# Forgetting attention's values in two 64-column halves for the low probabilities, memory values by 512 queries

## The chip, the cores and the metric

The kernel runs on one core of one Trainium2 chip. The metric is the device time of one execution in microseconds. Before the change it is 1254.17 us, the median of three runs (1252.7 to 1254.45).

## The reference

Two decoder layers over 1024 tokens of width 1024. Each layer projects its input once to a main branch, a memory query and two gates, mixes, and applies an output projection, a residual and a LayerNorm. Layer 0's main branch is causal pooling with windows 2, 4, 8 and 16 and a 256 x 256 map per group. Layer 1's is forgetting attention, 16 heads of 64 over keys, values and forget gates projected from its input. Both layers have 4-head cross-attention into 256 memory tokens.

```
# forgetting attention, per block of 128 queries
logits = einsum('bqhd,bkhd->bhqk', qi, k) * scale + (ci[..., :, None] - cum_k[:, :, None, :])
p = softmax(where(mask, logits, -inf))
out = einsum('bhqk,bkhd->bqhd', p, v)
# memory attention
p = softmax(einsum('bshd,bmhd->bhsm', q, mk) * MEM_HEAD_DIM ** -0.5)
out = einsum('bhsm,bmhd->bshd', p, mv)
# each layer
y = concatenate([y_main * silu(g_main), y_mem * silu(g_mem)]) @ w_out
x = layer_norm(ALPHA * x + y, g, b)
```

All inputs and outputs are f32.

## The kernel before

**Split operands.** Every f32 operand of a matmul is split into a high and a low part, and a product is taken in three matmuls: high by high, high by low, low by high. Projections use two f32r parts (`hi_lo`, L138). Attention probabilities and values use two f16 parts after scaling (`scaled_halves` L239 for values, `halves` L752 for probabilities), and the scale is undone when the result leaves PSUM (`undo`, `un`).

**Stages.** In order: pooling group 0 (`pool_group`, L488), memory keys and values of layer 0 (`mem_kv`), memory attention of layer 0 (`mem_attention`, L267), pooling groups 1 to 3, output projection and LayerNorm of layer 0, then for layer 1 memory keys, values and attention, `start_units` (the first head pairs' projections and the forget gates), the forgetting attention `fox` (L810), and the output projection.

**What sets the order on TensorE.** In the memory attention and in layer 1's attention the order of TensorE is the program's own (`manual_schedule`); the other engines are ordered by a scheduler. A projection is a generator (`slab`, L170) that yields after each matmul of 128 x 512; `Fill.pump(cols)` draws from such generators until the given number of columns has been issued. So attention work that waits for softmax stands between stretches of projection work. In `mem_attention` the fill is the four memory gates, in `fox` the gates and the next pairs' keys, queries and values.

**Memory attention.** For each step t (128 queries) `probs` makes the logits of four heads, softmax on VectorE and ScalarE, and a DMA transpose of the two f16 parts into `pt[t]` (tag "T", six buffers). `values(c, h)` covers 256 queries: for each of two tiles six matmuls (two blocks of memory tokens, three products), accumulated in a PSUM tile of tag "O" (h = 1) or "T", which VectorE scales into `ys[h]` (L324). It runs at t = 3, 5, 7, 9, with fill between the heads. At the end `ys` is multiplied by the gates (L338).

**Pooling.** After a group's two gates `pool_group` applies the group's map: four accumulators of 512 columns, six matmuls each, tag "pj" with two banks, the same that the gates before use. VectorE multiplies each by scale and gate (L530).

**Forgetting attention.** For each head the eight query tiles are done from the last to the first (`tile_of`). `probs` (L708) makes logits and exponentials of one tile, `halves` the two f16 parts one step later, and `turn` (L763) transposes them by DMA into `pt[hd, i]`: the first i + 1 blocks are the high part, the next i + 1 the low part. `values(hd, c, o)` (L773) runs LAG = 5 steps later, twice a head: c = 1 for tiles 4 to 7 (26 blocks of keys in all), c = 0 for tiles 0 to 3 (10 blocks). The weights `v[:, b, 2j : 2j + 2, :]` hold the 64 columns of V's high part beside the 64 of its low part. Each block is multiplied twice, by the high and by the low probabilities, so all four products are in one PSUM bank ("O", one buffer), 64 rows for V's high part and 64 for V's low part. ScalarE scales one half (L787), VectorE adds the other (L788). `VALUES` (L39) tells the pacing how many columns such a call takes, at which step of a head.

**`start_units`** (L686): 48 units of pair 0's projections (the key slab), `v_first` (values of the first two pairs and the forget logits, 192 matmuls at L606), the gates' VectorE work, transposes of values with 24 units between them, the rest of pair 0, then pair 1 with the two TensorE steps of the gates (L637 to L645).

Of the kernel before, what the change touches and what calls it, by code (L numbers as in the profile page):

```python
# [15 lines left out]
ALU = mybir.AluOpType  # L16
AX = mybir.AxisListType

P = 128
# [3 lines left out]
ST = S // P  # L23
NH = 512
HEADS = 16
MH = 4
# [9 lines left out]
LAG = 5  # L36
APART = 6 * NH
PSCALE = 2.0 ** 15
VALUES = {0: 52 * P, 4: 20 * P}  # L39


class Fill:
# [29 lines left out]
def trunk_kernel(ctx, tc, x, xT, memT, win, wk, wv0, wv, wmk, wmv, wout, poolw, pscale, lng, lnb, bforget, out):  # L72
# [28 lines left out]
    def ps(shape, tag, bufs):  # L101
        return psum.tile(shape, F32, tag=tag, name=nm(tag), bufs=bufs)
# [164 lines left out]
    def mem_attention(l, XH, XL, kv, qtile, ytile, yd):  # L267

        (kh, kl, v, undo), keys, vals = kv
        qs = []  # L270
        if l:
            for h in range(MH):
                keys(h)
        for h in range(MH):
            qh, ql = qtile(), qtile()
            run(slab(win[l, 8 + h], XH, XL, lambda cols, acc: hi_lo(qh[:, cols], ql[:, cols], acc)))
            qs.append((qh, ql))
            if not l:
                keys(h)
            vals(h)  # L280
        ys, gs = [ytile() for _ in range(MH)], [G() for _ in range(MH)]
        pt, fill = {}, Fill()
        for h in range(MH):
            fill.add(gate_units(win[l, 20 + h], gs[h], XH, XL), SLAB)

        def probs(i):

            p, two = sb([P, MH, NMEM], "P", 4), sb([P, 2, MH, NMEM], "P", 4, F16)
            m, ms, sm, r = tiny(MH), tiny(MH), tiny(MH), tiny(MH)
            for hp in range(2):  # L290
                lg = ps([P, 2, NMEM], "L", 3)
                for j in range(2):
                    h = 2 * hp + j
                    qh, ql = (t[:, i * P : (i + 1) * P] for t in qs[h])
                    mm3(lg[:, j, :], ((qh, kh[:, h, :]), (qh, kl[:, h, :]), (ql, kh[:, h, :])))
                pair = slice(2 * hp, 2 * hp + 2)
                nc.vector.tensor_reduce(m[:, pair], lg, AX.X, ALU.max, negate=True)
                nc.vector.tensor_scalar(ms[:, pair], m[:, pair], MSCALE, None, ALU.mult)
                for j in range(2):
                    h = 2 * hp + j  # L300
                    nc.scalar.activation(
                        p[:, h, :], lg[:, j, :], AF.Exp, bias=ms[:, h : h + 1], scale=MSCALE, accum_out=sm[:, h : h + 1],
                    )
            nc.vector.tensor_scalar(r, sm, 1.0 / PSCALE, None, ALU.mult)
            nc.vector.reciprocal(r, r)
            for h in range(MH):
                nc.scalar.activation(two[:, 0, h, :], p[:, h, :], AF.Copy, scale=r[:, h : h + 1])
                nc.vector.scalar_tensor_tensor(
                    two[:, 1, h, :], p[:, h, :], r[:, h : h + 1], two[:, 0, h, :], ALU.mult, ALU.subtract,
                )  # L310
            pt[i] = T([P, 2, MH, 2, P], F16)
            nc.sync.dma_start_transpose(
                pt[i].rearrange("p e h m q -> p (e h m) q"), two.rearrange("p e h t -> p (e h t)"),
            )

        def values(c, h):
            acc = ps([P, 2 * P], *(("O", 1) if h == 1 else ("T", 2)))
            for j in range(2):
                t = pt[2 * c + j]
                mm3(acc[:, j * P : (j + 1) * P], [  # L320
                    (v[:, h, 2 * e + m, :], t[:, f, h, m, :])
                    for m in range(2) for e, f in ((0, 0), (0, 1), (1, 0))
                ])
            nc.vector.tensor_scalar(ys[h][:, c * 2 * P : (c + 1) * 2 * P], acc, undo[:, h : h + 1], None, ALU.mult)  # L324

        with tc.manual_schedule(engines={PE}):
            for t in range(ST + 2):
                part = fill.left / (5 * (ST + 2 - t))
                if t < ST:
                    probs(t)  # L330
                fill.pump(part if t <= ST else 3 * part)
                for h in range(MH):
                    if t >= 3 and t % 2 == 1:
                        values((t - 3) // 2, h)
                    fill.pump(part if t <= ST else part / 2)
            fill.pump(float("inf"))
        for h in range(MH):
            nc.vector.tensor_tensor(ys[h], ys[h], gs[h], ALU.mult)  # L338
            nc.sync.dma_start(yd[:, h, :], ys[h])
# [143 lines left out]
    with tc.tile_pool(name="in0", bufs=1) as in0:  # L483

        def bt():
            return sb([P, S], "B", 8, F32R, in0)

        def pool_group(g):  # L488
            w = WINDOWS[g]
            pms = []  # L490
            for f in (2 * g, 2 * g + 1):
                u = sb([P, S], "P", 4)
                run(slab(
                    first[f] if g == 0 else win[0, f], XH, XL, lambda cols, acc: nc.scalar.copy(u[:, cols], acc),
                    ("L", 3) if f == 1 else ("pj", 2),
                ))
                cur, sh = u, 1
                while sh < w:
                    nxt = G()
                    nc.vector.tensor_tensor(nxt[:, sh:], cur[:, sh:], cur[:, : S - sh], ALU.add)  # L500
                    nc.vector.tensor_copy(nxt[:, :sh], cur[:, :sh])
                    cur, sh = nxt, 2 * sh
                pm = G()
                nc.vector.scalar_tensor_tensor(pm[:, w - 1 :], cur[:, w - 1 :], 1.0 / w, u[:, w - 1 :], ALU.mult, ALU.subtract)
                nc.vector.tensor_tensor(pm[:, : w - 1], cur[:, : w - 1], invc[:, : w - 1], ALU.mult)
                nc.vector.tensor_tensor(pm[:, : w - 1], pm[:, : w - 1], u[:, : w - 1], ALU.subtract)
                ph, pl = T(), T()
                hi_lo(ph, pl, pm)
                pms.append((ph, pl))
            r = raw([P, 2, 2 * P])  # L510
            nc.sync.dma_start(r, poolw[g])
            wh, wl = (MK([P, 2, 2 * P]) for _ in range(2))
            hi_lo(wh, wl, r)
            ys = []
            for f in (2 * g, 2 * g + 1):
                y = sb([P, S], "Y", 4, F32, in0)
                run(gate_units(win[0, 12 + f], y, XH, XL))
                ys.append(y)
            for d in range(2):
                f = 2 * g + d  # L520
                for n in range(2):
                    acc = ps([P, NH], "pj", 2)
                    terms = []
                    for ct in range(2):
                        a, b = wh[:, ct, d * P : (d + 1) * P], wl[:, ct, d * P : (d + 1) * P]
                        ph, pl = (t[:, n * NH : (n + 1) * NH] for t in pms[ct])
                        terms += [(a, ph), (a, pl), (b, ph)]
                    mm3(acc, terms)
                    yn = ys[d][:, n * NH : (n + 1) * NH]
                    nc.vector.scalar_tensor_tensor(yn, acc, pschalf[:, f : f + 1], yn, ALU.mult, ALU.mult)  # L530
                nc.sync.dma_start(y0d[f // 4, :, f % 4, :], ys[d])

        wtags = [("B", 8)] * 4 + [("W", 4)] * 2 + [("MK", 4)] * 2 + [("Y", 4)] * 2 + [("PG", 0), ("w", 0)]
        out_proj = OutProj(0, w_slots(wtags, in0), y0d)
        pool_group(0)
        kv = mem_kv(0)
        mem_attention(0, XH, XL, kv, bt, lambda: sb([P, S], "Y", 4, F32, in0), y0d[2])
        for g in range(1, 4):
            pool_group(g)
            out_proj.split((4, 12, 12)[g - 1])  # L540

        XH1, XL1 = (sb([P, KT, S], "A", 2, F32R) for _ in range(2))
        out_proj.rest(x, XH1, XL1, x1)
# [3 lines left out]
    with tc.tile_pool(name="in1", bufs=1) as in1:  # L547
# [137 lines left out]

        def start_units(own, following):  # L686

            yield from islice(own, 48)
            yield from v_first()
            gates = forget_gates()  # L690
            next(gates)
# [81 lines left out]
        def values(hd, c, o):  # L773

            (v, un), b = pairs[hd // 2][2], hd % 2
            acc = ps([P, NH], "O", 1)
            for i in range(4 * c, 4 * c + 4):
                mm3(
                    acc[:, (i % 4) * P : (i % 4) * P + P],
                    [  # L780
                        (v[:, b, 2 * j : 2 * j + 2, :].rearrange("p e d -> p (e d)"), pt[hd, i][:, e * (i + 1) + j, :])
                        for j in range(i + 1) for e in range(2)
                    ],
                )
            own, other = slice(64 * b, 64 * b + 64), slice(64 - 64 * b, P - 64 * b)
            oc = o[own, c * NH : (c + 1) * NH]
            nc.scalar.activation(oc, acc[other, :], AF.Copy, scale=un[own])  # L787
# [169 lines left out]
```

## Time and profile before

| | before |
|---|---|
| runs | 1254.17 us median of 3 (1252.7 to 1254.45) |
| profiled execution | 1252.11 us |
| its span, first to last instruction | 1250.3 us |
| granted TensorE clock over the span | 0.996 |
| matmuls, busy | 7018, 1234.2 us |
| of them values of the forgetting attention | 1152, 69.9 us |
| of them values of the memory attention | 384, 219 ns each |

PE is the matmul side of TensorE, PEld its weight loads, DVE VectorE, ACT ScalarE, POOL GpSimd, SP the queue that issues DMAs. A row of a group reads: line, engine, operation, output tile <- input tiles, shapes, count, then busy us and mean ns of one, then idle time of the engine just before them and what ended it. Matmuls overlap, so the duration of one is not its price; the price is the time from one start to the next.

### The profile page before, as it was taken

The numbers are of one execution on the slowest core, as the hardware profiler recorded it, in microseconds if no ns is written. First come the engines' busy times: TensorE is split into PE (matmuls) and PEld (weight loads), VectorE is DVE, ScalarE is ACT, GpSimd is POOL, SyncE is SP. The second block draws the span as 40 slices with busy tenths as digits, with TensorE's granted clock in tenths as the row PEclk, the third lists the DMA queues.
The fourth block names the chain that finished last, engine by engine and source line by source line (L and its number), as shares of the span: only waits on it lengthen the run. The fifth ranks groups of instructions, "written<-read, shape, count | busy, mean of one in ns | idle before, by whom it ended". The sixth has DMA issues, their size and how long they took to land.

```text
span 1250.3 us, 19605 instructions
## 1 busy us (share of the span) xinstructions
PE 1234.2 (99%) x7018; PEld 1038.3 (83%) x7018; DVE 793.7 (63%) x1869; ACT 569.1 (46%) x1241; POOL 171.1 (14%) x276
## 2 busy tenths in 40 slices
PE   9999999999999999999999999999999999999997
PEld 6888888888888888888897888888888888888885
DVE  6444766374644457357726888878877788775644
ACT  5233652242321123256424777767766677661110
POOL 0000000000000000000002343433334333430000
PEclk9999999999999999999999999999999999999998
DMA  6333544242363324234514778968887979884530
GB/s 227 100 103 87 124 110 138 90 118 86 101 219 118 118 93 135 71 106 108 173 52 129 167 171 183 185 165 177 180 185 153 196 186 213 228 242 160 175 106 34
DMA packets 267410, 178.64 MB, mean 143 GB/s; under 512 B 212273, under 2 KB 225713, under 8 KB 267313
## 3 DMA queue, kind: packets, MB, share of 16 engines
q1 hardware_dynamic: 267312, 177.40, 54.4%
q8 instruction: 55, 0.90, 0.3%
q14 instruction: 43, 0.34, 0.1%
HBM read 94.97 MB, written 22.61 MB: 94 GB/s over the span
## 4 chain that ended last, share of the span: by engine, by line
PE 94%; DVE 3%; DMA 1%; issue 0%; ACT 0%; POOL 0%; SPq 0%; DVEq 0%; POOLq 0%; ACTq 0%
PE pj L184 52%; PE L L388 9%; PE pj L388 9%; PE L L168 7%; PE O L168 6%; PE pj L217 3%; PE pj L606 2%; PE pj L168 1%; PE T L168 1%; PE T L388 1%; PE L L184 1%; PE O L388 1%; PE T L260 1%; DMA T<-P 1%; DVE w L142 0%
## 5 line engine op out<-in xcount | busy, mean ns | idle before, releaser
L184 PE MATMUL pj<-A,w 128*128 128x512 f32 x2928 | 709.4, 393 | 1.6 <-ACT A L141 1.6
L184 PEld LDWEIGHTS pj<-A,w 128*128 128x128 f32 x2928 | 540.3, 188 | 106.8 <-ACT A L141 2.5
L758 DVE SCALAR_TENSOR_TENSOR P<-T,s,P 128x512 f16<-128x512 f32 x192 | 111.7, 613 | 36.1 <-ACT P L757 35.1
L736 ACT ACTIVATE T<-MK,s 128x512 f32<-128x512 f32 x192 | 111.4, 580 | 46.6 <-DVE s L728 26.2
L142 DVE TENSOR_TENSOR w<-raw,w 128x512 fp32r<-128x512 f32 x106 | 73.8, 698 | 89.4 <-ACT w L141 88.9
L757 ACT ACTIVATE P<-T,s 128x512 f16<-128x512 f32 x192 | 102.9, 577 | 43.3 <-ACT T L736 18.2
L141 ACT CAST w<-raw 128x512 fp32r<-128x512 f32 x106 | 65.7, 621 | 114.5 <-PE pj L184 75.3
L168 PE MATMUL L<-B,B 128*128 128x512 f32 (+3 forms) x384 | 89.4, 341 | 0.7 <-DVE s L728 0.7
L633 POOL MEMSET G<- 128x128 f32 x1 | 0.2, 206 | 613.7 <-DVE V L338 613.7
L168 PEld LDWEIGHTS L<-B,B 128*128 128x128 f32 x384 | 70.6, 188 | 14.2 <-DVE s L728 1.1
L728 DVE CUSTOM_DVE_ANT_0 MK<-L,R 128x512 f32<-128x512 f32 (+3 forms) x128 | 72.7, 568 | 10.0 <-PE L L168 6.4
L168 PEld LDWEIGHTS <-V 128*128 128x128 f16 x1152 | 64.5, 98 | 9.2 <-issue 8.0
L142 DVE TENSOR_TENSOR T<-T,T 128x1024 fp32r<-128x1024 f32 x23 | 28.1, 1223 | 68.1 <-PE pj L388 49.9
L146 POOL TENSOR_TENSOR w<-raw,w 128x512 fp32r<-128x512 f32 x54 | 70.6, 1307 | 4.3 <-PE pj L184 0.5
L141 ACT CAST T<-T 128x1024 fp32r<-128x1024 f32 x23 | 24.2, 1052 | 101.9 <-DMA T<-y0d 52.1
L168 PE MATMUL O<-T,V 128*128 128x128 f16 x1152 | 69.9, 219 | 0.7 <-DMA T<-P 0.6
L720 POOL TENSOR_SCALAR_AFFINE_SELECT R<-R 128x128 f32<-128x128 f32 x128 | 42.1, 335 | 207.5 <-DVE s L728 161.5
L217 PE MATMUL pj<-T,w 128*128 128x256 f32 x384 | 48.9, 284 | 0.7 <-DVE s L444 0.4
L217 PEld LDWEIGHTS pj<-T,w 128*128 128x128 f32 x384 | 47.6, 191 | 2.0 <-DVE w L142 0.7
L388 PE MATMUL pj<-B,T 128*128 128x512 f32 x192 | 47.6, 389 | 0.0
L145 POOL TENSOR_SCALAR w<-raw 128x512 fp32r<-128x512 f32 x54 | 33.9, 628 | 89.8 <-PE pj L184 89.8
L388 PE MATMUL L<-B,T 128*128 128x512 f32 x168 | 43.3, 393 | 0.0
(208 smaller groups left out, 1584.4 us busy)
## 6 DMA issues: line engine op xcount, KB each, us to landing
raw<-in_win_dram SPq DMA_DIRECT2D x96, 256.0 KB, 2.8
raw<-in_wout_dram SPq DMA_DIRECT2D x40, 256.0 KB, 2.7
B<-B SPq DMA_DIRECT2D x32, 256.0 KB, 3.9
R<-cumd SPq DMA_DIRECT2D x16, 512.0 KB, 4.4
y0d<-Y SPq DMA_DIRECT2D x12, 512.0 KB, 2.6
T<-y0d SPq DMA_DIRECT2D x12, 512.0 KB, 3.9
T<-y1d SPq DMA_DIRECT2D x11, 512.0 KB, 4.1
raw<-in_wmk_dram SPq DMA_DIRECT2D x16, 256.0 KB, 2.6
```

Of the source, the lines that this page charges most:

```text
L141: pin(nc.scalar.copy(hi, src))
L142: pin(nc.vector.tensor_tensor(lo, src, hi.bitcast(F32), ALU.subtract))
L146: nc.gpsimd.tensor_tensor(lo, src, hi.bitcast(F32), ALU.subtract)
L168: nc.tensor.matmul(acc, a, b, start=i == 0, stop=i == len(terms) - 1)
L184: nc.tensor.matmul(accs[n], a[:, k, :], b[:, kt, n * NH : (n + 1) * NH], start=kt == 0 and i == 0, stop=kt == KT - 1 and i == 2,)
L217: nc.tensor.matmul(acc, w[:, k, :], m[pc][:, k, :], start=pc == 0 and k == 0 and i == 0, stop=pc == 1 and k == 3 and i == 2,)
L388: nc.tensor.matmul(accs[a][nh], y[:, k, a * P : (a + 1) * P], w, start=kt == 8 and i == 0, stop=kt == 7 and i == 2,)
L720: nc.gpsimd.affine_select(R[:, qs], R[:, qs], [[-1, P]], ALU.is_ge, -NEG, base=0, channel_multiplier=1).ins
L728: nc.vector.tensor_tensor_reduce(p[:, lo:up], lg, R[:, lo:up], 1.0, top, ALU.add, ALU.min, m[:, n : n + 1])
L736: nc.scalar.activation(e, p[:, lo:up], AF.Exp, bias=top, scale=-1.0, accum_out=sums[:, n, hd % 2, i : i + 1],)
L757: nc.scalar.activation(pair[:, lo:up], e, AF.Copy, scale=r)
L758: nc.vector.scalar_tensor_tensor(pair[:, L + lo : L + up], e, r, pair[:, lo:up], ALU.mult, ALU.subtract)
```

## The change

- In `fox`'s `values` the high probabilities are multiplied by both parts of V as before, first for all blocks of the call; then the low probabilities are multiplied by V's high part alone, with 64 columns of weights. These go in turn to PSUM rows 0 to 63 and 64 to 127, so that blocks of keys alternate between the two column halves of the array. The sum of both halves of the bank is what leaves it, as before. The product of low probabilities and V's low part is left out. Only the first matmul of a call clears the bank.
- `VALUES` becomes 39 and 15 times 128 columns.
- In `mem_attention`'s `values` one call covers 512 queries, one PSUM bank, and runs at t = 5 and t = 9. The fill is paced by a plan (`MVALUES` = 12,288 columns at these two steps), 40% after the logits and 15% after each head; at t = 5 and 9 the plan leaves no fill between the heads.
- `pool_group`'s four accumulators take tag "L" (three banks).
- `start_units` issues 24 units before `v_first` in place of 48.

```diff
-VALUES = {0: 52 * P, 4: 20 * P}
+MVALUES = MH * 4 * 6 * P
+VALUES = {0: 39 * P, 4: 15 * P}
...
         def values(c, h):
-            acc = ps([P, 2 * P], *(("O", 1) if h == 1 else ("T", 2)))
-            for j in range(2):
-                t = pt[2 * c + j]
+            acc = ps([P, NH], *(("O", 1) if h == 1 else ("T", 2)))
+            for j in range(4):
+                t = pt[4 * c + j]
...
             for t in range(ST + 2):
-                part = fill.left / (5 * (ST + 2 - t))
+                todo = [MVALUES if k in (5, 9) else 0 for k in range(t, ST + 2)]
+                part = max(0, (fill.left + sum(todo)) / len(todo) - todo[0])
                 if t < ST:
                     probs(t)
-                fill.pump(part if t <= ST else 3 * part)
+                fill.pump(part * 0.4)
                 for h in range(MH):
-                    if t >= 3 and t % 2 == 1:
-                        values((t - 3) // 2, h)
-                    fill.pump(part if t <= ST else part / 2)
+                    if todo[0]:
+                        values((t - 5) // 4, h)
+                    fill.pump(part * 0.15)
...
-                    acc = ps([P, NH], "pj", 2)
+                    acc = ps([P, NH], "L", 3)
...
-            yield from islice(own, 48)
+            yield from islice(own, 24)
...
             acc = ps([P, NH], "O", 1)
-            for i in range(4 * c, 4 * c + 4):
-                mm3(
-                    acc[:, (i % 4) * P : (i % 4) * P + P],
-                    [
-                        (v[:, b, 2 * j : 2 * j + 2, :].rearrange("p e d -> p (e d)"), pt[hd, i][:, e * (i + 1) + j, :])
-                        for j in range(i + 1) for e in range(2)
-                    ],
+            blocks = [(i, j) for i in range(4 * c, 4 * c + 4) for j in range(i + 1)]
+
+            def add(rows, i, j, e, last=False):
+                nc.tensor.matmul(
+                    acc[rows, (i % 4) * P : (i % 4) * P + P], v[:, b, 2 * j : 2 * j + (1 if e else 2), :].rearrange("p e d -> p (e d)"),
+                    pt[hd, i][:, e * (i + 1) + j, :], start=e == 0 and (i, j) == blocks[0], stop=last,
                 )
+
+            for i, j in blocks:
+                add(slice(0, P), i, j, 0)
+            for k, (i, j) in enumerate(blocks):
+                add(slice(64 * (k % 2), 64 * (k % 2) + 64), i, j, 1, k >= len(blocks) - 2)
```

More of the change, by code (lines that the diff above doesn't have):

```diff
@@ L323, in values @@
                 ])
-            nc.vector.tensor_scalar(ys[h][:, c * 2 * P : (c + 1) * 2 * P], acc, undo[:, h : h + 1], None, ALU.mult)
+            nc.vector.tensor_scalar(ys[h][:, c * NH : (c + 1) * NH], acc, undo[:, h : h + 1], None, ALU.mult)
         with tc.manual_schedule(engines={PE}):
             for t in range(ST + 2):
-                part = fill.left / (5 * (ST + 2 - t))
+                todo = [MVALUES if k in (5, 9) else 0 for k in range(t, ST + 2)]
+                part = max(0, (fill.left + sum(todo)) / len(todo) - todo[0])
                 if t < ST:
                     probs(t)
-                fill.pump(part if t <= ST else 3 * part)
+                fill.pump(part * 0.4)
                 for h in range(MH):
-                    if t >= 3 and t % 2 == 1:
-                        values((t - 3) // 2, h)
-                    fill.pump(part if t <= ST else part / 2)
+                    if todo[0]:
+                        values((t - 5) // 4, h)
+                    fill.pump(part * 0.15)
             fill.pump(float("inf"))
```

## The prediction, made before the changed kernel had run

> **What bounds the kernel now.** I read the page first: busy times, slices, the chain of work that ended last, groups.
>
> ```profile
> span 1250.3 us, 19605 instructions
> ...
> PE 1234.2 (99%) x7018; PEld 1038.3 (83%) x7018; DVE 793.7 (63%) x1869; ACT 569.1 (46%) x1241; POOL 171.1 (14%) x276
> ...
> PE   9999999999999999999999999999999999999997
> ...
> PEclk9999999999999999999999999999999999999998
> ...
> PE 94%; DVE 3%; DMA 1%; issue 0%; ACT 0%; POOL 0%; SPq 0%; DVEq 0%; POOLq 0%; ACTq 0%
> ```
>
> TensorE is busy in every slice at its full clock, and 94% of the chain is its own matmuls. A modelled busy share alone would not prove that, so the second view is what TensorE itself waited for:
>
> ```profile
> engine line waited for: us in total, times, longest us
> ...
> PE pj L168 <- DVE Y L198: 1.4, 3, 0.5
> ...
> PE L L168 <- DVE s L728: 0.7, 1, 0.7
> PE O L168 <- DMA T<-P: 0.6, 1, 0.6
> PE pj L606 <- DVE B L660: 0.4, 1, 0.4
> ...
> PE O L637 <- DVE G L629: 0.3, 1, 0.3
> ```
>
> No wait is above 1.6 us in total. So the time is the sum of TensorE's pitches (start to start of successive matmuls), and the change is worth what it takes off that sum. The third view, the stretch of the forgetting attention by engine, says how much room the others leave (us of 400: PE, PEld, DVE, ACT, POOL, then clock, DMA share, GB/s):
>
> ```profile
> 700.00:1100.00 400.00, 399.29 (x2631) 338.31 (x2630) 319.37 (x919) 284.79 (x659) 149.58 (x240) 1.00 0.84 184
> ```
>
> VectorE has 20% left there, ScalarE 29%.
>
> **The forgetting attention's values.** These are the two groups to change, and one call of `values` with the work on either side of it, in order of time (start, length, what):
>
> ```profile
> L168 PE MATMUL O<-T,V 128*128 128x128 f16 x1152 | 69.9, 219 | 0.7 <-DMA T<-P 0.6
> ...
> L168 PEld LDWEIGHTS <-V 128*128 128x128 f16 x1152 | 64.5, 98 | 9.2 <-issue 8.0
> ```
> ```profile
> 805.91 0.42 PE L184 MATMUL pj<-A,w 128*128 128x512 f32 x1
> 806.17 3.08 PE L168 MATMUL O<-T,V 128*128 128x128 f16 x52
> 809.06 1.05 PE L168 MATMUL L<-B,B 128*128 128x512 f32 x4
> ```
>
> A matmul row lasts 219 ns, but 52 of them last 3.08 us: (3.08 - 0.22) / 51 = 56 ns pitch, weight load included. All 1152 (16 heads, 36 blocks, high and low probabilities) cost 64.5 us. The change leaves the 576 of the high probabilities as they are and makes the 576 of the low ones 64 columns wide, alternately in the left and the right half of the array. Their count and their 128 moving rows each stay; the gain exists only if the two halves run at the same time.
>
> No row of this trace shows a 64-column matmul. Bounds from the nearest rows:
> - Best: two halves take one pitch. The low pass falls from 576 x 56 = 32.3 us to 16.1: 16.1 us saved.
> - No gain: loads set the pitch, one after another. The nearest rows for a load-bound stream are the forget gates' running sums, whose moving side shrinks to 16 columns while each load stays 128 wide:
>
> ```profile
> 666.15 0.46 PE L637 MATMUL O<-G,G 128*128 128x128 f32 x2 [0.35 <-DVE G L629]
> 666.45 1.63 PE L639 MATMUL O<-G,G 128*128 128x112 f32 x14
> ```
> ```profile
> 666.34 1.64 PEld L639 LDWEIGHTS O<-G,G 128*128 128x128 f32 x14
> ```
> ```profile
> L639 PEld LDWEIGHTS O<-G,G x14: 192/192/192, 666.3 to 667.8; 128*128 128x128 f32 x14
> ```
>
>   Fourteen loads in 1.64 us, the last 0.19: (1.64 - 0.19) / 13 = 112 ns for an f32 load of 128 columns, whatever the matmul. Half the columns at that rate are 56 ns: in series, exactly today's pitch, and nothing is saved.
> - Worst: such a load isn't hidden behind the matmul before it, 56 + 56 = 112 ns each: 576 x 56 = 32 us lost.
>
> I take the first, since f16 loads of full width already keep inside 56 ns (98 ns long, 52 in a run without a gap) and two half loads are together no wider than one of them.
>
> The Trainium skill, TensorE: Matmul & The Clock Gate (section Measured speedup vs the span model), reports 2.38 times for three column tiles of 32; by the same share of the ideal two would run 1.59 times as fast, an estimate by which the saving would be 12 us and not 16. No run here shows it.
>
> Second, the array changes its width twice a call: 16 heads x 2 calls x 2 = 64 changes. From below: nothing, as today's change from f16 to f32r weights (the first f32r matmul at 809.06, the last f16 one ends at 806.17 + 3.08 = 809.25) doesn't wait for the matmuls in flight. From above: the next one starts only when the last has ended, 219 - 56 = 163 ns, and its load (98 ns) is exposed too: 261 ns, 16.7 us in all. I take the 163 ns, 10.4 us: a change of the array's shape is more than a change of data type, but a load has somewhere to go while the last matmul drains. Net: -16.1 + 10.4 = -5.7 us.
>
> The Trainium skill, TensorEngine Tiling (Array Packing), section Key Properties, says that changing the tiling mode drains the engine. This trace has one mode only and cannot show it; without a drain the sum would be 10.4 us lower, and that is a rival below.
>
> The order inside a call changes too: all high blocks, then all low. The first matmul still needs block 4c, the youngest transposed tile, so the DMA that it waits for is the same and as late. Evacuations (L787, L788) read the same bank with the same scale, and its next use is four steps later. Nothing goes to another queue. `VALUES` (52 to 39, 20 to 15 columns of 128) only spreads the same projection units a little differently over a head's steps: nothing, as long as the other engines keep their 20%.
>
> **The memory values.** The same 12 matmuls per 256 queries and head, but 24 in a row for 512 queries, the four heads back to back, and no gate projections in between.
>
> ```profile
> 159.99 1.17 PE L184 MATMUL pj<-A,w 128*128 128x512 f32 x4
> 161.00 0.84 PE L168 MATMUL O<-T,MK 128*128 128x128 f16 x12
> 161.66 1.17 PE L184 MATMUL pj<-A,w 128*128 128x512 f32 x4
> 162.67 0.84 PE L168 MATMUL T<-T,MK 128*128 128x128 f16 x12
> ```
> ```profile
> 520.38 10.91 PE pj L184 x48
> ```
>
> One turn, 161.00 to 162.67, is 1.67 us; its work is 12 x 56 ns and 4 x 227 ns (10.91 us / 48), 1.58 us. The passage between the two kinds costs 0.09 us. Sixteen passages a layer become two: 14 x 0.09 x 2 layers = -2.5 us. What this could uncover: a third accumulator in "T" waits for the first one's evacuation. It is two heads (2.7 us) behind it, and the 256-column evacuation takes 0.48, so even twice that is covered by those 2.7 us. The oldest probabilities (`pt[3]`, `pt[7]`) are two steps old when read, as before. The eight 512-column evacuations in place of sixteen lie on VectorE, which has time.
>
> ```profile
> L324 DVE TENSOR_SCALAR Y<-O,undo x4: 454/482/489, 147.3 to 189.9; 128x256 f32<-128x256 f32 x4
> ```
>
> **The pooling's map** moves its accumulators from "pj" (two banks, still held by the gates of the slab before) to "L" (three, idle then):
>
> ```profile
> 52.10 1.52 PE L168 MATMUL pj<-T,MK 128*128 128x512 f32 x6
> 54.07 2.11 PE L168 MATMUL pj<-T,MK 128*128 128x512 f32 x8 [0.45 <-DVE Y L198]
> ```
>
> Six matmuls from 52.10 would end their pitches at 53.46; the next starts at 54.07: 0.6 us, three times by the waits: -1.8 us.
>
> **`start_units`** puts v's projection 24 units earlier and those 24 behind it. The waits at L606 (0.4) and L637 (0.3) lose their cause: the bank is no longer just filled, and the gates' VectorE work gets 24 x 0.227 = 5.4 us more. The later steps of the gates stand behind the same count of matmuls, so the wait for the row of forget sums (part of L728's 0.7) stays. -0.7 us.
>
> **Sum:** -5.7 - 2.5 - 1.8 - 0.7 = -10.7 us. The profiled execution took 1252.1 us (1250.3 of span and 1.8 around it), 2.1 us below the median of the runs. Against it the sum is 1241.4; against the median of 1254.2 it is 1243.5, say 1244.
>
> **The rivals.** The three small edits (-5.0) are in each of them.
> - *Full overlap and free changes:* -16.1 - 5.0, 1233. For it: the f16/f32r passage that drains nothing. Against it: that passage keeps the array whole. Chance 0.15.
> - *Narrow loads in series (slower):* in the low pass a load becomes the pitch, 56 ns as worked out, and the 64 changes are paid for nothing: +10.4 - 5.0 = +5.4, 1260. It decides from a low pitch of 56 - 5.4 / 0.576 = 46.6 ns on. For it: the running sums, where loads visibly set the pitch; against: f16 loads are faster than those today. Chance 0.28.
> - The Trainium skill, TensorEngine Tiling (Array Packing), section Restrictions, says that column tiling disables the fast weight load; that would put the narrow f16 loads at the running sums' rate, which is this rival's mechanism, if both halves share one load path.
> - *Loads not hidden at all:* 112 ns, +32.3 + 10.4 - 5.0: 1292. The 64.5 us of today's runs without a gap speak against it. Chance 0.06.
> - *Another engine takes over in the forgetting attention:* VectorE with its 80% is late at some steps and the 5.7 us become waits at L728: only the small edits remain, 1249. Chance 0.06, since 6 us in 400 raise its share by one point.
>
> **How the numbers follow.** The forecast (overlap, paid drains) has 0.45. Its own range is 1237 (changes at 60 ns) to 1250 (changes at 261 ns). No change means within 0.2%, 2.5 us, about what measuring this kernel can tell. Faster: 0.43 of the forecast, 0.15 and 0.03 of the last rival, 0.61. Within: 0.02, 0.03 and 0.03 of a series case with cheap changes, 0.08. Slower: 0.31. The range for 8 in 10 runs from the full overlap to the series case with changes between 163 and 261 ns: 1232 to 1265.
>
> **What would show it.** In the trace after, a low pass of 26 matmuls takes about 26 x 28 = 0.73 us from first to last start, and the gap before its first and after its last start is about 0.16 us above the pitch; starts of a pair lie close together. A low pitch near 56 is the series rival, near 112 the unhidden one; no gap at the change is the full overlap. TensorE's waits at L530's bank, L606 and L637 are gone, and the memory values stand as runs of 96 f16 matmuls. New waits of TensorE for VectorE in the forgetting attention would be the last rival. I am wrong if the low pitch is above 47 ns.

## The result, and the profile after

| | before | after |
|---|---|---|
| runs | 1254.04 us median of 4 (1252.7 to 1254.45) | 1238.81 us median of 4 (1238.09 to 1241.55) |
| profiled execution | 1252.11 us | 1239.22 us |
| its span | 1250.3 us | 1237.5 us |

The ratio is 0.9888 (95% interval 0.9874 to 0.9903): faster by about 1%. Measured again later beside the kernel before (`changed_again` below), it was 0.9901 (0.9887 to 0.9916). By these the gain lies between 10 and 16 us; profile against profile it is 12.9. The forecast was 10.7.

Of those 12.9 us, 1.9 are not the change's. The profiled execution of the kernel before waited longer for its first operands (1.6 us behind ScalarE's L141, after the change 0.9), and its granted clock was 0.51 from 8.0 to 11.3 us, where the kernel after had 1.00: its 41st projection matmul starts at 17.64 us, that of the kernel after at 15.76. From that matmul to the end of the span the kernel after is 10.9 us shorter.

The page of the kernel after, in its first lines and the rows of the values:

```profile
span 1237.5 us, 19607 instructions
...
PE 1222.9 (99%) x7018; PEld 1026.7 (83%) x7018; DVE 788.8 (64%) x1853; ACT 567.4 (46%) x1241; POOL 170.9 (14%) x276
...
L782 PEld LDWEIGHTS <-V 128*128 128x128 f16 (+1 forms) x1152 | 49.3, 104 | 12.3 <-issue 8.4
L782 PE MATMUL O<-T,V 128*128 128x128 f16 (+1 forms) x1152 | 57.7, 221 | 0.3 <-DMA T<-P 0.2
```

The same count of matmuls; TensorE is still the bound, and the values' busy time fell from 69.9 to 57.7 us although each row is as long as before (221 against 219 ns): rows now lie on top of each other. What TensorE waited for, after (us in total, times, longest):

```profile
PE L L169 <- DVE s L730: 2.5, 1, 2.5
...
PE pj L185 <- ACT A L142: 0.9, 1, 0.9
PE pj L218 <- DVE s L446: 0.4, 1, 0.4
...
PE O L782 <- DMA T<-P: 0.2, 1, 0.2
```

The waits of the pooling's map, of v's projection and of the forget gates are gone in this execution, as forecast. That of v's projection is not always gone: the same kernel in `changed_again` has 0.3 us of it (L608 there, 0.4 before). One wait grew: at L730, for the first row of forget sums, from 0.7 to 2.5 us.

Two calls of the forgetting attention's values in order of time (start, length, what), first a short and a long one after, then a short one before; the long one of before stands in the prediction.

```profile
784.08 1.13 PE L782 MATMUL O<-T,V 128*128 128x128 f16 x20
785.14 1.67 PE L185 MATMUL pj<-A,w 128*128 128x512 f32 x6
...
798.29 2.47 PE L782 MATMUL O<-T,V 128*128 128x128 f16 x52
800.70 0.73 PE L185 MATMUL pj<-A,w 128*128 128x512 f32 x2
```
```profile
792.04 1.29 PE L168 MATMUL O<-T,V 128*128 128x128 f16 x20
793.14 1.64 PE L184 MATMUL pj<-A,w 128*128 128x512 f32 x6
```

From a call's first matmul to the next work's first: the long call took 2.89 us (806.17 to 809.06) and takes 2.41; the short one took 1.10 and takes 1.06. If two narrow blocks share one pitch of 56 ns, the long call has 26 + 13 = 39 pitches, 2.18 us, and 0.23 us over them; the short one 15 pitches, 0.84 us, and 0.22 over. The excess is the same in both, so it belongs to the two changes of width and not to the blocks. The single starts, which the views merge, show it as such: the two matmuls of a pair start 3 or 4 ns apart, the next pair 52 or 53 ns later (76 or 77 after the first pair), and 149 ns lie between the starts on either side of a change, 93 over the pitch. Counting also the f32r matmul behind the call, the median long call falls by 0.461 us and the short one by 0.014: 16 x 0.475 = 7.6 us for the forgetting attention. With its 13 pairs a long call gains 0.73 and pays 0.27 for its two changes, 0.13 each; a short one, with 5 pairs, pays back nearly all.

The memory values after, with four heads in a row between two stretches of logits:

```profile
156.77 1.59 PE L169 MATMUL L<-MK,B 128*128 128x256 f32 x12
158.20 1.51 PE L169 MATMUL T<-T,MK 128*128 128x128 f16 x24
159.55 1.50 PE L169 MATMUL O<-T,MK 128*128 128x128 f16 x24
160.89 2.84 PE L169 MATMUL T<-T,MK 128*128 128x128 f16 x48
163.54 1.67 PE L169 MATMUL L<-MK,B 128*128 128x256 f32 x12
```

96 matmuls in 163.54 - 158.20 = 5.34 us, 56 ns each, nothing between the heads. And the pooling's map:

```profile
50.21 5.60 PE L169 MATMUL L<-T,MK 128*128 128x512 f32 x24
55.65 0.62 PE L185 MATMUL pj<-A,w 128*128 128x512 f32 x2
```

24 matmuls in 5.44 us, 227 ns each, without the stop of 0.6 us after the sixth, and without a second one of 0.11 us that the kernel before made in each of three groups.

### The profile page after: what moved, and what is told of

It is laid out like the page before. It is cut to its first block, busy times and chain, and to the rows that moved or that the text cites. A ratio compares the mean times of both kernels' runs of the same rounds, so it can differ in the third digit from the quotient of the medians.

```text
span 1237.5 us, 19607 instructions
## 1 busy us (share of the span) xinstructions
PE 1222.9 (99%) x7018; PEld 1026.7 (83%) x7018; DVE 788.8 (64%) x1853; ACT 567.4 (46%) x1241; POOL 170.9 (14%) x276
## 5 line engine op out<-in xcount | busy, mean ns | idle before, releaser
L759 ACT ACTIVATE P<-T,s 128x512 f16<-128x512 f32 x192 | 103.0, 577 | 42.4 <-ACT T L738 19.8
L730 DVE CUSTOM_DVE_ANT_0 MK<-L,R 128x512 f32<-128x512 f32 (+3 forms) x128 | 72.5, 567 | 13.3 <-PE L L169 6.9
L782 PEld LDWEIGHTS <-V 128*128 128x128 f16 (+1 forms) x1152 | 49.3, 104 | 12.3 <-issue 8.4
L782 PE MATMUL O<-T,V 128*128 128x128 f16 (+1 forms) x1152 | 57.7, 221 | 0.3 <-DMA T<-P 0.2
L390 PE MATMUL pj<-B,T 128*128 128x512 f32 x192 | 47.6, 389 | 0.0
L302 ACT ACTIVATE P<-L,s 128x256 f32<-128x256 f32 x64 | 29.5, 474 | 29.8 <-DVE s L299 28.1
```

The source lines that it names most:

```text
L390: nc.tensor.matmul(accs[a][nh], y[:, k, a * P : (a + 1) * P], w, start=kt == 8 and i == 0, stop=kt == 7 and i == 2,)
L730: nc.vector.tensor_tensor_reduce(p[:, lo:up], lg, R[:, lo:up], 1.0, top, ALU.add, ALU.min, m[:, n : n + 1])
L759: nc.scalar.activation(pair[:, lo:up], e, AF.Copy, scale=r)
L782: nc.tensor.matmul(acc[rows, (i % 4) * P : (i % 4) * P + P], v[:, b, 2 * j : 2 * j + (1 if e else 2), :].rearrange("p e d -> p (e d)"), pt ...
```

## The experiments

The kernels ran in three sets, each beside the kernel before on the same chip; the ratio to it is the number to compare between sets. The kernel before had a median of 1251.96, 1252.19 and 1252.12 us in the three sets.

**One half of the change each.** `fox_values_only` is the kernel before with the new forgetting attention values and `VALUES`; `small_edits_only` is the kernel after without them.

> The kernel before with the forgetting attention's values of the change alone (the 64-column low pass and VALUES). Theory: two halves run as one pitch and each of the 64 changes of width costs 0.13 us, so a long call falls by 0.46 us and a short one by 0.01, 8 us in all with the DMA wait that one call had: 1246. Rival (most of the gain comes from the small edits, and the values' part is used up by waits in the forgetting attention): 1250 or more.

> The change without its forgetting attention part: memory values by 512 queries, the pooling's map in L, 24 units. The prediction's terms give -5.0: 1249. Theory after the trace: the stages give -0.8 and -0.7 (memory), -2.3 and about -0.6 (pooling), and nothing from start_units, where 1.1 us are won and lost again in a wait for the forget sums: 1249.5. Rival (all that the values' part doesn't explain of 15.2 us is theirs): 1247.

Measured: 1246.84 us, 0.9956 (0.9943 to 0.9969), and 1246.48 us, 0.9955 (0.9939 to 0.9971). About 5.5 us each, and in their profiled executions 7.8 and 6.2 us of span (1242.5 and 1244.1 against 1250.3). The calls of `fox_values_only` are those of the changed kernel to the nanosecond (2.520 and 1.180 us; this is from the f32r matmul ahead of a call to the second one behind it, less the pitches of two f32r matmuls, 227 ns each; before it was 2.981 and 1.194). Both expectations were reckoned from 1254 us, as -8 and -4.5.

By the medians the first half gave 5.1 us, less than the 8 expected (which lies outside the interval of 3.9 to 7.1), the second 5.5. The medians don't settle the rivals: 4 us or less for the first half is at the edge of its interval, and 7 us for the second inside its own (3.6 to 7.6). The traces do. In `fox_values_only` no wait uses up what the calls gain: 0.5 us for transposed tiles, and 1.6 us at L728 where the kernel before has 0.7. Counted from the 41st projection matmul on, so without the unlike starts (17.64 us before, 15.72 and 15.89 here), the spans are 5.9 and 4.5 us shorter, 10.3 together; the changed kernel's two profiles are 10.9 and 10.3 us shorter. So the halves add. The memory and pooling edits had no run each of their own; what each gives is read from its stage in the traces.

**Is it the overlap of the two halves?** `low_in_one_half`:

```diff
-                add(slice(64 * (k % 2), 64 * (k % 2) + 64), i, j, 1, k >= len(blocks) - 2)
+                add(slice(0, 64) if k < len(blocks) - 1 else slice(64, P), i, j, 1, k >= len(blocks) - 2)
```

> The changed kernel with all low blocks but the last of a call in the left half of the array. Theory (the gain is the overlap of two halves; one half alone keeps the pitch of 56 ns): a long call has 12 pitches of 56 ns more, a short one 4: 16 x (0.67 + 0.22) = +14.3 us, 1253. Rival 1 (a 64-column matmul is cheap by itself): 1239. Rival 2 (a load into a half waits for the matmul in the same half, 112 ns): +14 +30, 1283.

Measured: 1253.86 us, 1.0021 (1.001 to 1.0032). The same two calls in its timeline:

```profile
789.67 1.35 PE L782 MATMUL O<-T,V 128*128 128x128 f16 x20
790.95 1.65 PE L185 MATMUL pj<-A,w 128*128 128x512 f32 x6
...
803.99 3.14 PE L782 MATMUL O<-T,V 128*128 128x128 f16 x52
807.06 0.72 PE L185 MATMUL pj<-A,w 128*128 128x512 f32 x2
```

1.28 and 3.07 us: 0.22 and 0.66 over the changed kernel, which is 4 and 12 pitches of 56 ns. A narrow matmul alone costs a whole pitch; the gain is that two in different halves share it. The width changes remain with hardly any gain, and the kernel is slower than before. By the ratios it lies 15 to 17 us above the changed kernel, where its calls explain 14.1. In the profile most of the rest is another thing: the wait at L730 was 3.1 us (2.5 in the kernel after), and the granted clock 0.69 in the 5 us from 675 to 680 around its end.

**Is it the order, high blocks first?** `low_full_width` gives the low pass its 128 columns back, after the high pass; `low_full_planned` also puts `VALUES` back to 52 and 20.

```diff
-                    acc[rows, (i % 4) * P : (i % 4) * P + P], v[:, b, 2 * j : 2 * j + (1 if e else 2), :].rearrange("p e d -> p (e d)"),
+                    acc[rows, (i % 4) * P : (i % 4) * P + P], v[:, b, 2 * j : 2 * j + 2, :].rearrange("p e d -> p (e d)"),
...
-                add(slice(64 * (k % 2), 64 * (k % 2) + 64), i, j, 1, k >= len(blocks) - 2)
+                add(slice(0, P), i, j, 1, k == len(blocks) - 1)
```

> The changed kernel with the low pass at 128 columns (V's low part in it again), still after the high pass. Theory: the pairs and the changes of width are both gone, a long call is back at 2.98 us, a short one at 1.19: +7.6 us, 1246.5, and the trace has no pitch of 149 ns around the low pass. Rival (the order of the passes or the pacing carries the gain): 1240.

> The low pass at 128 columns after the high pass, as before, but with VALUES back at 52 and 20. Theory: the 8 us over 1246.5 that the last one showed come from the plan: with 39 and 15 for calls that take 52 and 20 pitches the late gate products reach the output projection late, TensorE stands still there for 3 us and its clock falls. With a plan that fits, 1246.5, and no wait at L390. Rival (the order, all high blocks first, costs 8 us by itself): 1254.

Measured: 1254.31 us, 1.0015 (1.0002 to 1.0028), and 1248.61 us, 0.9966 (0.9954 to 0.9978). In both the calls are back at 2.981 and 1.194 us, so the order carries nothing in the calls. But the first was 8 us above what I expected. Its waits of TensorE begin with one that the kernels above don't have:

```profile
PE L L390 <- ACT T L142: 2.7, 1, 2.7
```

That is the output projection waiting for its first gated outputs. With the plan that fits the call's length this wait is gone (a second one of 0.5 us at L390, behind DVE, stands in both kernels). The kernel is then 6 us faster, near `small_edits_only` and 2 us above the 1246.5 expected, and `VALUES` is not the detail for which the prediction took it.

**Where the change of width stands.** `all_narrow` makes the high pass narrow too (high by high in the left half, high by low in the right), so that the width changes at the two ends of a call and not in its middle; `low_first_in_long_calls` exchanges the passes in calls of 26 blocks. The new lines of the first, which take the place of `add` and its two loops:

```diff
+            todo = [(i, j, 0, part) for i, j in blocks for part in range(2)] + [(i, j, 1, 0) for i, j in blocks]
+            for k, (i, j, e, part) in enumerate(todo):
+                rows = slice(64 * (k % 2), 64 * (k % 2) + 64)
+                nc.tensor.matmul(
+                    acc[rows, (i % 4) * P : (i % 4) * P + P], v[:, b, 2 * j + part, :],
+                    pt[hd, i][:, e * (i + 1) + j, :], start=k < 2, stop=k >= len(todo) - 2,
+                )
```

> The changed kernel with its high pass in 64 columns too: high by high in the left half, high by low in the right, then the low pass. As many pitches (39 and 15 a call), and the array changes its width at the two ends of a call alone, not in its middle. Theory (a change costs 0.13 us wherever it stands): two changes a call as before, the same within 1.5 us. Rival 1 (a change at the passage from f32r work is dearer, as that matmul takes longer to drain, 0.16 us): +1 to +2 us. Rival 2 (loads of three half blocks in place of two instructions a block are too many to issue): a pair takes more than 56 ns, +5 us or more.

> The changed kernel with the low pass ahead of the high pass in the calls of 26 blocks. Theory: two changes of width, now at the start and in the middle, the same price: within 0.7 us of the changed kernel. Rival (the change at the end is dear because the f32r loads behind it wait too, 0.207 us over the pitches against 0.118 in the middle): 16 x 0.1 = 1.6 us less.

> The changed kernel itself once more, beside the others of this set. If the parts add as the traces say (7.8 and 6.2 us of 1250.3), it is 14 us under the kernel before of this set, ratio 0.989; if they add as the medians of the two parts say (0.9956 x 0.9955), 11 us, 0.991.

Measured: `all_narrow` 1247.46 us, 0.9953 (0.9939 to 0.9967); `low_first_in_long_calls` 1241.7 us, 0.9909 (0.9893 to 0.9924); the changed kernel beside them 1240.44 us, 0.9901 (0.9887 to 0.9916). In the single starts the change costs 91 to 96 ns over the pitch (of 56 ns, or of 227 behind an f32r matmul) in every place: f32r to narrow, narrow to f32r, full to narrow, narrow to full. What a place adds is the f32r load behind it: the next f32r matmul follows after 0.34 us when narrow work ended the call and after 0.31 when full-width work did. So the calls of `all_narrow` are slightly shorter than the changed kernel's (2.501 and 1.161 us) and the long calls of the second kernel shorter still (2.463); rivals 1 and 2 of `all_narrow` fall. For the passes exchanged, the place of the change does matter, as the rival had it, but by 0.9 us (16 x 0.057) and not 1.6, and the median doesn't show it: it is 1.3 us above the changed kernel's, inside the intervals.

The median of `all_narrow` is 7 us above the changed kernel's, where "the same within 1.5 us" was expected. In its profiled execution, the fastest of its runs with 1243.77 us, the place is the output projection again:

```profile
1107.77 1.43 PE L390 MATMUL pj<-B,B 128*128 128x512 f32 x5
1111.54 3.34 PE L390 MATMUL L<-B,T 128*128 128x512 f32 x6 [2.34 <-ACT T L142]
1114.67 1.59 PE L390 MATMUL L<-w,T 128*128 128x512 f32 x6
```
```profile
1110.00:1115.00 5.00, 3.43 (x8) 2.27 (x9) 3.49 (x5) 2.77 (x4) 0.00 (x0) 0.66 0.75 282
1115.00:1120.00 5.00, 5.00 (x24) 4.13 (x23) 2.35 (x4) 1.39 (x3) 1.43 (x2) 1.00 0.90 300
```

The wait is 2.3 us, and then six matmuls take 3.13 us in place of 1.39, as the granted clock (the third number from the end) is 0.66 in these 5 us: against the changed kernel's pace these six begin 2.5 us late and take 1.7 us longer. That is 4 of the 7 us; its other executions left no trace, so whether they lost more in the same place is not shown. The DMA queue shows why, first in the changed kernel, then in `all_narrow`:

```profile
1099.65 1.18 SPq L423 DMA_DIRECT2D T<-y1d  x1
1101.10 0.40 SPq L814 DMA_DIRECT2D y1d<-R  x1
1101.59 3.69 SPq L364 DMA_DIRECT2D raw<-in_wout_dram  x4
1105.33 0.52 SPq L423 DMA_DIRECT2D T<-y1d  x1
```
```profile
1101.47 0.33 SPq L810 DMA_DIRECT2D y1d<-R  x1
1101.90 3.76 SPq L364 DMA_DIRECT2D raw<-in_wout_dram  x4
1105.75 0.58 SPq L423 DMA_DIRECT2D T<-y1d  x1
```

The load of the first gated outputs (L423) stands ahead of a store and four weight loads in the one and behind them in the other, some 6 us later. No edit moved it: the scheduler orders this queue, and with another TensorE call it chose another order. `low_full_width` and `low_full_planned` have the late order too; in the second TensorE comes to these matmuls at 1117.72, 6.4 us after that load was issued, and waits only the 0.5 us behind DVE. That this order alone makes the difference was not tried with the order set by hand.

**The two settings beside the values.** `units_48` is the changed kernel with 48 units ahead of v's projection, `plan_52_20` the changed kernel with the old `VALUES`.

> The changed kernel with 48 units ahead of v's projection as before. Theory after the trace (24 units win about 1 us in that projection and lose as much in the later wait for the forget sums): within 1 us of the changed kernel. The prediction's term: +0.7.

> The changed kernel with VALUES at 52 and 20 as before. Theory (the plan only spreads the same units; VectorE and ScalarE have room): the same within 1 us, and the last load of the gated outputs stays ahead of the weights' loads in the queue, so no wait at L390. Rival (a plan that doesn't fit costs at the passage to the output projection, as with the low pass at full width): +3 to +6 us and a wait at L390.

Measured: 1241.12 us, 0.9912 (0.9899 to 0.9926): not to be told from the changed kernel (0.9901), as the trace said, and not from the prediction's +0.7 either. Its trace has the two waits back (0.9 us at L608, 0.4 at L639) and 1.6 us at L730. And 1244.28 us, 0.9939 (0.9926 to 0.9951): 3 to 4 us worse than `units_48` and the changed kernel, as much as the rival had, but not where it had it. There is no wait at L390; two calls of values wait, one until ScalarE's high parts (L759), one for a transposed tile:

```profile
PE O L782 <- ACT P L759: 2.2, 1, 2.2
PE O L782 <- DMA T<-P: 1.4, 1, 1.4
```

A plan that reckons the call too long holds fill back at the value steps. Before these two calls TensorE goes from the logits straight to the values, where the changed kernel (`changed_again`) has one projection matmul between and waits 0.4 us at one of the two. That fits, but one matmul of 0.23 us is not 2.2 us; how the rest comes about is not shown.

**A faster version.** The gates' VectorE chain ends (L631 starts at 652.06) long before its first TensorE step (658.75), so that step can go earlier, and the load of the first row of forget sums with it.

```diff
-            yield from own
-            yield from islice(following, 9)
-            next(gates)
-            yield from islice(following, 9)
-            next(gates)
-            yield from islice(following, 30)
+            yield from islice(own, 33)
+            next(gates)
+            yield from islice(own, 9)
+            next(gates)
+            first_R.append(forget_rows(0))
+            yield from own
+            yield from islice(following, 48)
...
-            ahead_R = forget_rows(0)
+            ahead_R = first_R.pop()
```

> The changed kernel with the forget gates' two TensorE steps 24 units earlier and the load of the first row of forget sums right behind them, before the forgetting attention starts. The trace of the changed kernel has the gates' VectorE chain done 6.4 us before its first TensorE step, and a wait of 2.5 us at the second tile's logits for that row. Theory: the wait goes, 1.9 to 2.5 us less than the changed kernel of the last set (1240.4): 1238. Rival (the row waits for the DMA queue and the 16 engines, not for the sums): no change.

> The same with the low pass first in the long calls, which took 0.057 us off each of the 16 in the trace: another 0.9 us, 1237. Rival (the medians of the last set, where it was 1.3 us slower than the changed kernel, mean more than its calls): 1239.5.

Measured: 1239.17 us, 0.9894 (0.9881 to 0.9908), and with the low pass first in long calls 1237.63 us, 0.9883 (0.987 to 0.9897). The wait at L730 is gone in both; what is left for TensorE in the second is

```profile
PE pj L185 <- ACT A L142: 1.3, 1, 1.3
...
PE O L783 <- DMA T<-P: 0.7, 2, 0.4
```

and its long call takes 2.28 us from first matmul to the next work (797.80 to 800.08) against 2.41:

```profile
797.80 2.47 PE L783 MATMUL O<-T,V 128*64 128x128 f16 x52
800.08 0.71 PE L185 MATMUL pj<-A,w 128*128 128x512 f32 x2
```

It has the lowest median of all kernels here, but its interval overlaps the changed kernel's. Beside `gates_earlier` it is 1.5 us lower, beside the changed kernel of the set before 2.8 us lower. The medians alone don't settle the rivals: the first step was 1.3 us where 1.9 to 2.5 were expected, the second 1.5 where the trace gave 0.9, and alone it had been 1.3 us the other way. Against "no change" for the first step speaks that the wait is gone. Its profiled span, 1238.2, is not below the changed kernel's 1237.5, but it had the slow start of the kernel before (the 41st projection matmul at 17.67 us); from there on it is 1.2 us shorter than the changed kernel's first profile, and that of the second kernel 3.5 us.

## Why the prediction was right

**The mechanism** is the forecast's: halves overlap, changes of width cost. The pair of low blocks takes one pitch, 56 ns, which is the 16.1 us of the first term: two halves together do twice what one does. `low_in_one_half` takes apart 12 of the 13 pairs of a long call and 4 of the 5 of a short one, and its calls are longer by just those pitches, 14.1 us in all. Loads in series and loads not hidden are both excluded by the same rows.

**The changes of width** were mis-sized: I took 163 ns, the whole of a matmul's row over its pitch. It is 93 over the pitch in the starts, 0.13 us a change with what the first pair and the f32r matmuls behind it lose. 64 x 0.03 = 2 us more gain than forecast: -7.6 in place of -5.7. The next matmul starts 149 ns after the last of the old width, while that one's row lasts 219 ns: the row's end was the upper side of a bound and not its likeliest place. The Trainium skill, TensorEngine Tiling (Array Packing), section Key Properties, has a change of tiling mode drain the engine; the 91 to 96 ns that a change adds, in every direction, agree with a drain, though the trace shows the gap alone and not what fills it; the page gives no number for it.

**The memory values**, -2.5: right, it was -2.4. From the first memory logits to the last values layer 0 went from 66.71 to 65.92 us, with two gate matmuls (0.45) more in it: 1.2 us a layer, and as much in layer 1.

**The pooling's map**, -1.8: it was -2.4. I took the three waits that the view lists, 0.61 us each; each of these three groups stopped a second time for 0.11 us, and the fourth lost 0.12, and these stops are under the view's threshold.

**`start_units`**, -0.7: at most that, and given back. Its wait at L637 went; that at L606 went in the profile after, but in six of the other profiles with 24 units 0.2 to 0.3 us of it are left. The wait for the forget sums grew by 1.8 us in the profile; over the other profiles with 24 units, where the gates were not moved, it was 1.2 to 3.1 us, and over the three with 48 units 0.7 and twice 1.6. So part of the growth is the spread of one DMA's landing between executions, and what remains for the edit, under 1 us, is not settled. I had held that the wait stays, and had not counted that spread. `gates_earlier` takes the wait away.

**`VALUES`**, nothing: wrong. Left at 52 and 20 it would have cost 3 to 4 us (`plan_52_20`); the plan had to follow the calls.

**What no term has.** The stretch up to the end of pooling group 0 was 2.6 us shorter, 0.75 of it the map. The other 1.9 are the start told with the result, a longer wait and a lower clock in one execution; `fox_values_only`, which has the old map, is 1.9 us shorter there too. In the profiles the terms sum to -7.6 - 2.4 - 2.4 - 0.7 + 1.8 - 1.9 = -13.2, against -12.8 of span.

**How near the number is, and why.** Without that start the terms that belong to the change sum to -11.3, against 10.9 measured and 10.7 forecast. That these lie so close is in part luck: the changes of width and the map gave 2.5 us more than forecast, and the wait for the forget sums took 1.8 back.

**The rivals.** Full overlap with free changes is excluded by the 149 ns, series loads by the pair's 56 ns, another engine by the waits: none of TensorE for VectorE in the forgetting attention but the one for the first row.

## What to carry to other kernels

Narrow weights pay in pairs, one in each half, and a run of pairs has to be long enough for its two changes of width: here each pair gains 56 ns and the changes of one run cost 0.27 us, so five pairs only break even. Where a hand-written plan paces filler work around a call, its cost there has to change with the call; where a scheduler orders a queue, look after every edit whether a load that TensorE will want has moved behind others.

## What the runs showed that I had not expected

- A wait of TensorE of 2.3 us came with a granted clock of 0.66 over 5 us (`all_narrow`), and cost 1.7 us more by the clock. The wait of 2.5 us at L730 in the kernel after came with no such loss (clock 1.00 from 670 to 680), the one of 3.1 us at the same place in `low_in_one_half` did (0.69 over 5 us), and so did one of 1.4 us near the start of the kernel before (0.51 over 3.3 us). So in these traces the length of a wait alone doesn't tell whether the clock falls.
- Kernels that differ in the calls of values (one also in `VALUES`) got two different orders of one DMA queue, three of them the later place for a load that TensorE needs. In `all_narrow` 4 us were lost there, half of the change's own gain in the forgetting attention.
- The Trainium skill, TensorEngine Tiling (Array Packing), section Restrictions, says that column tiling disables the fast weight load. In the changed kernel a load of 64 columns lasts 109 ns on the mean, one of 128 columns 98, so half the columns take no less time; this is in keeping with the page. But they set no pitch here: two of them and two matmuls fit in 56 ns.
